# Score products behind another unit's value products, norm weights as a column of x, and a second DMA queue at the start of a streaming-encoder step

## The chip, the cores and the metric

The kernel runs on one core of one Trainium2 chip. The metric is the device time of one execution in microseconds (us); lower is better. The time before is the median of three runs.

## The reference, cut to what matters

One step of a one-layer hybrid encoder: 512 prompt rows and 32 sample rows (544 together) of width 1024, 256 memory tokens, and caches for the sample rows. Three groups of heads, A, B and M, take their queries, keys, values and gates from one input projection, and one output projection joins them.

```python
def _mixer_inputs(x, g, w_in, pos):
    z = _rmsnorm(x, g) @ w_in                       # 1024 x 3880
    qa, ka, va, ga, qb, kb, vb, gb, qm, gm, qi, ki, wi = _split_cols(z)
    qb, kb = _rope(qb, pos), _rope(kb, pos)         # qi, ki too
    return ...

def _attend(q, k, v, bias):                         # A: band + bias; M: memory
    s = jnp.einsum('bqhd,bkhd->bhqk', q, k) * ATTN_SCALE + bias
    return jnp.einsum('bhqk,bkhd->bqhd', jax.nn.softmax(s, axis=-1), v)

def _indexer_scores(qi, ki, wi):                    # B: which keys
    dots = jnp.einsum('bqhd,bsd->bqhs', qi, ki) * (D_IDX ** -0.5)
    return jnp.einsum('bqh,bqhs->bqs', wi * (H_IDX ** -0.5), jax.nn.relu(dots))

def _gather_attend(q, k, v, scores, topk):          # B: over the top-k keys
    top_val, top_idx = lax.top_k(scores, topk)
    ...

def _merge(x, oa, ob, om, ga, gb, gm, w_out):
    o = jnp.concatenate([oa * jax.nn.silu(ga), ob * jax.nn.silu(gb), om * jax.nn.silu(gm)], axis=-1)
    return x + o @ w_out                            # then a last _rmsnorm
```

A and B have six heads of 64 columns, M has four; the indexer has eight heads of 32 and one shared key. B picks 128 keys for a prompt row and 256 for a sample row.

## The kernel before, in words

**Precision and products.** Everything is float32. A large product is made of three products of rounded parts: ACT rounds a block of weights to `wh`, DVE or POOL subtracts to get `wl`, the same is done for x (`xTh`, `xTl`), and TensorE (PE) adds `wh·xTh`, `wl·xTh` and `wh·xTl` in one bank of PSUM. So every block of weights passes through SP's DMA queue (a tile `raw`), ACT (`wh`), and POOL or DVE (`wl`) before PE can use it.

**Stages.** The start loads x turned around (`x_t`, eight blocks of 128 rows by 544 columns) and the first columns of `w_in` (the indexer's, 296 wide, as `raw`), block beside block, in `x_load`, lines 861 to 881. `x_split`, lines 897 to 919, multiplies x by the norm weights `g_mix` and splits it. PE fills the time until the first blocks are there with products of a tile `ones`. `ahead_load` and `ahead_split`, lines 816 to 837, do the same for the block of keys `ka0`. Then the blocks of the input projection follow in the order of `EARLY` and `LATE`. Between them lie the attention units: A's three pairs of heads, M's two, B's three. The output projection comes last, first with the rows of A and M (`oAh`, `oAl`, `oMh`, `oMl`), then with those of B (`oBh`, `oBl`), with the residual (`residual`, line 2139) and the final norm (`settle`, lines 2164 to 2197) behind each block.

**A unit of attention** (`attend`, lines 1986 to 2014) makes the parts of its queries and keys (`q`, `ql`, `k`, `kl`), the scores `k·q`, the softmax in tiles `z`, turns them with PE (`ident`), multiplies by the values (`mix`, `z·va` or `z·vb`), and hands the result on. Scores and value products use PE's array divided into parts of half its rows or columns, as do the sample rows' products with the raw weights (`raw,oS`), which `out_sample`, lines 1709 to 1731, issues; `out_rows` adds their results to `xrS` on DVE.

**What sets the order.** A planner runs while the program is built. It keeps a model of all engines (`Line`), and generators in a heap issue the instructions at modelled times; the order on each engine is fixed from then on. Every instruction passes through `Timed.call`, line 411, so all rows of the profile carry that line, and the tiles' names tell them apart. Three rules matter here. `divided(k, issue)`, lines 491 to 512, collects groups of products for the divided array: a group that is alone waits up to `HOLD` for a second, then all that wait are issued together. A unit takes its places for `z` (`SCORES`, nine in all) before it prepares its keys, and gives them back after its value products:

```python
        yield from line.wait(lambda: places[0] >= k)
        places[0] -= k
        ...
        sc = yield from divided(k, u.begin)
        ...
        o = yield from divided(1, lambda: u.mix(bank()))
        places[0] += k
```

And the subtraction for `wl` goes to POOL unless POOL stands more than 0.5 later than DVE in the model. `START` is the order of the first loads ("x" blocks of x, "w" of weights, "t" the tables, "r" rows of x, "m" memory).

Of the kernel before, what the change touches and what calls it, by code (L numbers as in the profile page):

```python
# [36 lines left out]
START = "xxxwwwwtrrrrrwmmrr"  # L37
SURE = 1.0
SLACK = 1.06
HOLD = 2.0  # L40
LAG = 0.3
# [3 lines left out]
EARLY = ("va", "ka1", "ka2", "mk", "mv", "qa0", "qa1", "ga0", "qa2", "ga1", "ga2", "qm0", "gm0", "qm1", "gm1")  # L45
AHEAD = "ka0"
LATE = ("gb0", "kb0", "kb1", "qb0", "qb1", "kb2", "qb2", "vb", "gb1", "gb2")
# [46 lines left out]
class Line:  # L94
# [4 lines left out]
    def __init__(self):  # L99
        self.clk = {"PE": 1.35, "DVE": 0.7, "ACT": 0.9, "POOL": 1.2, "SP": 0.7}  # L100
# [60 lines left out]
    @staticmethod  # L161
    def lag(of, to):

        if of is None and to == "PE":
            return 0.3
        if of == to or of is None:
            return 0.127 if to == "DVE" else 0.09 if to == "POOL" else 0.0
        return 0.95 if of == "SP" else 0.26 if to == "PE" else 0.2 if of == "PE" else 0.06 if of == "POOL" else 0.15
# [69 lines left out]
    def rate(self):  # L238

        t = self.clk["SP"]  # L240
        return 340e3 if t < 1 else 170e3 if t < 2.3 else 330e3 if t < 7 else 310e3 if 11 < t < 22 else 370e3

    def op(self, eng, op, outs, ins, kw):
# [16 lines left out]
        d = (outs[0].size() * 4 / self.rate() if eng == "SP" else  # L260
# [33 lines left out]
    def begin(self, o, t):  # L294
        last = self.last
        o.start = t
        if o.eng == "SP":
            o.end = max(t + 1.3, last["DMA"]) + o.d
            o.after = {"SP": t + 0.45, "DMA": o.end}
# [12 lines left out]
        self.clk[o.eng] = o.end if o.eng != "SP" else t  # L312
# [29 lines left out]
    def sure(self, *tiles):  # L342

        return When(lambda: max(self.had(x) for x in tiles), SURE + (0.0 if self.now() < 40 else 0.0))
# [95 lines left out]
def hybrid_step(ctx: ExitStack, tc: tile.TileContext, a: dict):  # L440
# [3 lines left out]
    V, G, A, PE, DMA = (Timed(line, n, e) for n, e in (("DVE", nc.vector), ("POOL", nc.gpsimd), ("ACT", nc.scalar),  # L444
                                                       ("PE", nc.tensor), ("SP", nc.sync)))
# [44 lines left out]
    def divided(k, issue):  # L490
# [3 lines left out]
        job = [k, issue, None, False]  # L494
        waiting.append(job)
        end = line.now() + HOLD
        while not job[3]:
            if len(waiting) == 1 and line.now() < end:
                yield min(end, line.soon())
                continue  # L500
# [3 lines left out]
            for j in [job] + [j for j in waiting if j is not job]:  # L504
                if there(j[0]):
# [136 lines left out]

    def w_split():
        for i in range(len(w_list)):
# [26 lines left out]
            if i < 4:  # L671
                for kk in range(2):
                    yield line.at(raw[:, kk, :])
                    rounded(wh[:, kk, :], raw[:, kk, :])
                    yield line.at(wh[:, kk, :]) - 0.2
# [7 lines left out]
            tsub(V if i in WV or 0.5 < line.clk["POOL"] - line.clk["DVE"] else G, wl, raw, f(wh))  # L683
# [124 lines left out]
    gT = [cp.tile([P, NK], F32, name=n) for n in ("g_mix", "g_mem")]  # L808
# [7 lines left out]
    def ahead_load():  # L816
# [3 lines left out]
        DMA.dma_start(raw, w_in[k0 * P:k1 * P, c0:c0 + P].rearrange("(k p) n -> p k n", p=P))  # L820
# [4 lines left out]
    def ahead_split():  # L825
        for c, (k0, k1) in enumerate(CHUNKS):
# [9 lines left out]
            tsub(V if c else V, wl, raw, f(wh))  # L836
# [24 lines left out]
    def x_load():  # L861
# [3 lines left out]
        t = (rp.tile([P, 2, N], F32, tag="xr", name="xr", bufs=3) if c < 3 else  # L865
             cp.tile([P, 2, N], F32, tag="gate1", name="xr"))
# [30 lines left out]
    def x_split():  # L897
        for c in range(NK // 2):
            yield from line.wait(lambda: len(x_raw) > c)
            t = x_raw[c]  # L900
            for kk in range(2):
                yield line.at(t[:, kk, :], gT[0])
                k = 2 * c + kk
                h, l = xTh[k // 4][:, k % 4, :], xTl[k // 4][:, k % 4, :]
                if k < 1:
                    for j in range(2):
                        sl = slice(j * N // 2, (j + 1) * N // 2)
                        yield line.at(t[:, kk, :])
                        A.activation(h[:, sl], t[:, kk, sl], AF.Copy, scale=gT[0][:, k:k + 1])
                        x_half[0] += 1  # L910
                    yield line.at(h) - 0.2
                    V.scalar_tensor_tensor(l, t[:, kk, :], gT[0][:, k:k + 1], f(h), op0=ALU.mult, op1=ALU.subtract)
                else:
                    yield from part(h, l, t[:, kk, :], gT[0][:, k:k + 1])
# [3 lines left out]
            G.tensor_tensor(xF[:, k, :], t[:, :, S:N], gT[0][:, k].unsqueeze(2).broadcast_to([P, 2, T]), op=ALU.mult)  # L918
# [1370 lines left out]
```

## Time and profile before

| what | value |
|---|---|
| median of 3 runs | 340.26 us (340.23 to 340.39) |
| the profiled execution | 340.1 us |
| its span | 338.3 us |
| mean granted clock of PE | 0.998 |
| busy share | PE 98%, DVE 84%, ACT 65%, POOL 49% |
| instructions in the span | 7679 |

The profile is of one execution. Busy time is in us and as a share of the span; the slices cut the span in 40 equal parts, with a digit for tenths of busy time. Weight loads of PE have a row of their own, PEld, and overlap its products. A row of the timeline gives start, length, engine, line, operation, tile written and tile read, and how many instructions it groups; a bracket at its end names the engine's idle time just before it and what ended it. A product's modelled end overlaps the next one's start, so the distance of two starts tells what one takes.

### The profile page before, as it was taken

How to read it: one execution, taken by the hardware profiler on the slowest of the kernel's cores; microseconds unless marked ns; L12 is line 12 of the kernel's file. 1: busy time of each engine (PE TensorE's matmuls, PEld its weight loads, DVE VectorE, ACT ScalarE, POOL GpSimd, SP SyncE). 2: the span in 40 equal slices, each digit the busy share in tenths (PEclk: the TensorE clock that was granted, in tenths of full speed). 3: DMA queues.
4: the chain of work that ended last, by engine and by line, in shares of the span. 5: the costliest groups of instructions: out<-in, count | busy, mean ns of one | idle time of the engine just before them, and what ended most of it. 6: DMA issues, size and time to landing. Idle time of an engine off the chain costs nothing.

```text
span 338.3 us, 7679 instructions
## 1 busy us (share of the span) xinstructions
PE 329.9 (98%) x2785; PEld 296.4 (88%) x2785; DVE 283.2 (84%) x726; ACT 219.9 (65%) x523; POOL 166.1 (49%) x191
## 2 busy tenths in 40 slices
PE   8999999999999999999999999999999999999992
PEld 8979997999998989998999999899998776878682
DVE  3957878698989999699999999999979899865762
ACT  5838787898758786776776755532469446864362
POOL 2326261585453389246257764685338513361542
PEclk9999999999999999999999999999999999999999
DMA  7999763176539412314113343141332977002033
GB/s 219 382 302 344 202 219 105 33 216 160 157 84 304 143 58 58 94 37 136 49 33 74 103 140 97 48 117 42 98 127 65 334 296 273 0 2 95 0 114 152
DMA packets 44725, 46.61 MB, mean 138 GB/s; under 512 B 4400, under 2 KB 36720, under 8 KB 44688
## 3 DMA queue, kind: packets, MB, share of 16 engines
q1 hardware_dynamic: 44688, 46.13, 44.0%
q8 instruction: 22, 0.36, 0.4%
q14 instruction: 15, 0.12, 0.1%
HBM read 39.95 MB, written 6.16 MB: 136 GB/s over the span
## 4 chain that ended last, share of the span: by engine, by line
PE 80%; DVE 9%; issue 4%; POOL 3%; ACT 2%; DMA 1%; POOLq 0%; DVEq 0%; ACTq 0%
PE bank L411 80%; DVE gate L411 1%; DVE ysel L411 1%; DVE m L411 1%; DVE xr L411 1%; DMA raw<-in_w_mem_kv_dram 1%; DVE z L411 1%; DVE KSs L411 1%; POOL wl L411 1%; DVE rot L411 1%; POOL wI L411 1%; POOL rot L411 1%; DVE bi L411 0%; ACT junk L411 0%; POOL rs L411 0%
## 5 line engine op out<-in xcount | busy, mean ns | idle before, releaser
L411 POOL TENSOR_TENSOR wl<-raw,wh 128x512 fp32r<-128x512 f32 (+1 forms) x65 | 90.7, 1398 | 107.3 <-ACT wh L411 105.5
L411 PE MATMUL bank<-xTh,wh 128*128 128x272 f32 x352 | 77.0, 299 | 0.1
L411 ACT ACTIVATE wh<-raw 128x512 fp32r<-128x512 f32 (+3 forms) x85 | 52.0, 619 | 37.2 <-PE bank L411 11.8
L411 PE MATMUL bank<-xTh,wl 128*128 128x272 f32 x352 | 73.0, 288 | 0.0
L411 PE MATMUL bank<-xTl,wh 128*128 128x272 f32 x352 | 72.8, 288 | 0.0
L411 PEld LDWEIGHTS bank<-xTh,wh 128*128 128x128 f32 x352 | 55.6, 189 | 5.2 <-issue 4.1
L411 ACT ACTIVATE z<-z,st 128x128 f32<-128x128 f32 (+3 forms) x78 | 41.0, 549 | 22.9 <-DVE st L411 22.9
L411 PEld LDWEIGHTS bank<-xTh,wl 128*128 128x128 f32 x352 | 55.2, 189 | 0.6 <-issue 0.6
L411 PEld LDWEIGHTS bank<-xTl,wh 128*128 128x128 f32 x352 | 55.2, 188 | 0.5 <-issue 0.5
L411 PE MATMUL bank<-wh,xTh 128*128 128x384 f32 (+1 forms) x88 | 26.9, 336 | 0.0
L411 DVE MAX8 m<-ysel 128x8 f32<-128x256 f32 (+2 forms) x48 | 26.4, 550 | 0.1
L411 PE MATMUL bank<-wh,xTl 128*128 128x384 f32 (+1 forms) x88 | 26.2, 327 | 0.0
L411 PE MATMUL bank<-wl,xTh 128*128 128x384 f32 (+1 forms) x88 | 26.1, 326 | 0.0
L411 DVE MATCH_REPLACE8 ysel<-m,ysel 128x256 f32<-128x256 f32 (+2 forms) x48 | 26.0, 542 | 0.0
L411 DVE SCALAR_TENSOR_TENSOR ysel<-r,wI,ysel 128x256 f32<-128x256 f32 (+2 forms) x21 | 18.6, 885 | 4.2 <-ACT r L411 3.6
L411 ACT ACTIVATE junkS<-ysS,bi 128x1056 int8<-128x1056 f32 x16 | 18.7, 1168 | 4.2 <-DVE bi L411 4.1
L411 PE MATMUL bank<-ident,z 128*128 128x128 f32 (+1 forms) x162 | 21.2, 272 | 0.0
L411 PEld LDWEIGHTS bank<-ident,z 128*128 128x128 f32 (+1 forms) x162 | 17.8, 141 | 2.0 <-issue 0.7
L411 ACT COPY z<-bank 128x512 f32<-128x512 f32 (+2 forms) x31 | 15.2, 517 | 5.5 <-PE bank L411 3.9
L411 ACT ACTIVATE r<-bank 128x512 f32<-128x512 f32 (+3 forms) x30 | 14.0, 485 | 5.8 <-PE bank L411 5.0
L411 PEld LDWEIGHTS bank<-wh,xTh 128*128 128x128 f32 x88 | 15.8, 191 | 0.4 <-issue 0.4
L411 PEld LDWEIGHTS bank<-wl,xTh 128*128 128x128 f32 x88 | 15.7, 188 | 0.0
(286 smaller groups left out, 765.1 us busy)
## 6 DMA issues: line engine op xcount, KB each, us to landing
raw<-in_w_in_dram SPq DMA_DIRECT2D x42, 256.0 KB, 2.9
raw<-in_w_out_dram SPq DMA_DIRECT2D x16, 256.0 KB, 4.1
raw<-in_w_in_dram SPq DMA_DIRECT2D x8, 384.0 KB, 4.0
xr<-in_x_t_dram SPq DMA_DIRECT2D x8, 272.0 KB, 4.3
nat<-in_x_prompt_dram SPq DMA_DIRECT2D x4, 512.0 KB, 5.4
raw<-in_w_mem_kv_dram SPq DMA_DIRECT2D x8, 256.0 KB, 3.1
xr<-in_x_prompt_dram SPq DMA_DIRECT2D x4, 512.0 KB, 6.3
out_dram<-xr SPq DMA_DIRECT2D x4, 512.0 KB, 2.6
```

The costliest lines, as they stand in the source:

```text
L411: return fn(*args, **kw)
```

## The change: what it does

**The start.** `norm_mix_g` is no tensor of its own any more: it stands as a 545th column beside x's 544 in `x_t`, and the scalings read it there. The first `raw` block and the first block of `ka0` are issued on ACT's DMA queue (`DMA2`), not SP's. The first two blocks of x are split in two halves, and the second half of the first one waits until the first `wh` is issued.

**Scores behind value products.** `divided` takes a condition `may`. A unit prepares its queries and keys without having its places; its scores then wait in `divided` until the places are there, and the places are given back when the value products are issued. With `LINK`, value products that scores wait for do not hold for company, and the scores go out right behind them.

**The model and the lists.** The planner gets the second queue and other rates for it; `HOLD` is 3.0, `LAG` 0.5, `SCORES` 8, the margin in the first 40 us 1.5; `EARLY` and `LATE` list the blocks in another order; the sample rows' choice waits for the prompt's picks.

**Engines.** The second half of the rotary step of turned blocks, the subtraction for A's `kl`, and that of `ka0`'s later blocks go to POOL; a `wl` goes to DVE only where POOL is 5.0 later.

```diff
-START = "xxxwwwwtrrrrrwmmrr"
+START = "xxxtwwwwrrrrrwmmrr"
-HOLD = 2.0
-LAG = 0.3
+LINK = True
+HOLD = 3.0
+LAG = 0.5
-LATE = ("gb0", "kb0", "kb1", "qb0", "qb1", "kb2", "qb2", "vb", "gb1", "gb2")
+LATE = ("gb0", "kb1", "qb0", "kb0", "gb1", "qb1", "vb", "qb2", "gb2", "kb2")
...
-    def divided(k, issue):
+    def divided(k, issue, may=lambda: True):
...
-        job = [k, issue, None, False]
+        job = [k, issue, None, False, may]
         while not job[3]:
-            if len(waiting) == 1 and line.now() < end:
+            if not may():
+                yield line.soon()
+                continue
+            if sum(j[4]() for j in waiting) == 1 and line.now() < end and not (LINK and any(j[0] and not j[4]() for j in waiting)):
                 yield min(end, line.soon())
                 continue
...
-                if there(j[0]):
+                if there(j[0]) and j[4]():
...
-            tsub(V if i in WV or 0.5 < line.clk["POOL"] - line.clk["DVE"] else G, wl, raw, f(wh))
+            tsub(V if i in WV or 5.0 < line.clk["POOL"] - line.clk["DVE"] else G, wl, raw, f(wh))
...
-        DMA.dma_start(raw, w_in[k0 * P:k1 * P, c0:c0 + P].rearrange("(k p) n -> p k n", p=P))
+        (DMA if ahead else DMA2).dma_start(raw, w_in[k0 * P:k1 * P, c0:c0 + P].rearrange("(k p) n -> p k n", p=P))
...
-            tsub(V if c else V, wl, raw, f(wh))
+            tsub(G if c else V, wl, raw, f(wh))
...
                 DMA.dma_start(t[:, kk, :], a["x_t"][rows, :])
-                DMA.dma_start(gT[0], a["norm_mix_g"])
-            DMA.dma_start(raw[:, kk, :], w_in[rows, QI:QI + 296])
+            (DMA if c + kk else DMA2).dma_start(raw[:, kk, :], w_in[rows, QI:QI + 296])
...
-                if k < 1:
+                if k < 2:
                     for j in range(2):
...
+                        if k == 0 and j:
+                            yield from line.wait(lambda: w_k[0] or wh_0)
...
-            V.tensor_tensor(t, t, ctab["sin64"][:, sl], op=ALU.mult)
+            G.tensor_tensor(t, t, ctab["sin64"][:, sl], op=ALU.mult)
             yield line.at(t, out) - 0.2
-            least(out, V, G).tensor_tensor(out, t, out, op=ALU.add)
+            G.tensor_tensor(out, t, out, op=ALU.add)
...
-    SCORES = 9
+    SCORES = 8
...
-        yield from line.wait(lambda: places[0] >= k)
-        places[0] -= k
...
-        sc = yield from divided(k, u.begin)
+        def begin():
+            places[0] -= k
+            return u.begin()
+
+        sc = yield from divided(k, begin, lambda: places[0] >= k)
...
-        o = yield from divided(1, lambda: u.mix(bank()))
-        places[0] += k
+        def mix():
+            places[0] += k
+            return u.mix(bank())
+
+        o = yield from divided(1, mix)
...
-        pair = Pair(0, hp, lambda hp=hp: both(split_q(queried[0][:, hp, 0:S], 1.0, G), split_of(natural["ka"][:, hp, 0:S], 1.0, V, "k")), lambda: va)
+        pair = Pair(0, hp, lambda hp=hp: both(split_q(queried[0][:, hp, 0:S], 1.0, G), split_of(natural["ka"][:, hp, 0:S], 1.0, G, "k")), lambda: va)
```

Since the planner sets the order, three places show how it moves. First ACT at the very start of the program, before; `m_73` is a scratch tile, `xTh_79` the rounded x:

```order
L411 ACT_TABLE_LOAD
L411 ACTIVATE m_73<-nhalf 128x1
L411 ACTIVATE xTh_79<-xr,g_mix 128x272 x2
L411 ACTIVATE wh<-raw 128x296
L411 ACTIVATE wh<-raw 128x128
L411 ACTIVATE wh<-raw 128x296
```

ACT at the same place in the changed program:

```order
L412 DMA raw<-in_w_in_dram 128x296
L412 DMA raw<-in_w_in_dram 128x128
L412 ACT_TABLE_LOAD
L412 ACTIVATE m_73<-nhalf 128x1
L412 ACTIVATE xTh_79<-xr 128x272
L412 ACTIVATE wh<-raw 128x296
L412 ACTIVATE xTh_79<-xr 128x272
L412 ACTIVATE wh<-raw 128x128
```

Two loads now stand ahead of all else on ACT, `g_mix` is no longer read, and the first `wh` stands between the two halves of x.

Second PE in the last third of the program, where B's value products (`z,vb`) go out among the blocks of the output projection (`wh,oAh` and its like); before:

```order
L411 MATMUL bank<-wh,oAh 128x512
L411 MATMUL bank<-wh,oAl 128x512
L411 MATMUL bank<-wl,oAh 128x512
L411 MATMUL bank<-z,vb 64x128 x20
L411 MATMUL bank<-wh,oAh 128x512
```

PE at the value products of the same unit in the changed program; `ident,z` turns a softmax tile, `k,q`, `k,ql` and `kl,q` are the next unit's scores:

```order
L412 MATMUL bank<-ident,z 128x128 x4
L412 MATMUL bank<-raw,oS 32x512 x4
L412 MATMUL bank<-z,vb 64x128 x20
L412 MATMUL bank<-k,q 128x128 x2
L412 MATMUL bank<-k,ql 128x128 x2
L412 MATMUL bank<-kl,q 128x128 x2
L412 MATMUL bank<-k,q 128x256 x2
L412 MATMUL bank<-k,ql 128x256 x2
L412 MATMUL bank<-kl,q 128x256 x2
L412 MATMUL bank<-k,q 128x384 x2
```

The unit's value products stood alone between whole-array products; now sample products stand ahead of them and the next unit's scores right behind. Over the whole program whole-array products are left for a divided form 39 times before and 33 times after; the unbroken pieces of one divided form are 49 before and 45 after; whole products follow something else 62 times in both.

Third DVE near the end, where it adds PE's last blocks to the residual (`xr` with a number is one block of 128 rows, `xrS` the sample rows, `ss` the sums of squares, `gf` the weights of the last norm); before:

```order
L411 TENSOR_TENSOR xrS<-bank,xrS 32x512
L411 TENSOR_SCALAR ss<-ss 32x1
L411 TENSOR_TENSOR xr_3872<-bank,xr_3872 128x512
L411 SCALAR_TENSOR_TENSOR xrS<-xrS,ss,gf 32x512
L411 TENSOR_TENSOR xr_3873<-bank,xr_3873 128x512
L411 SCALAR_TENSOR_TENSOR xr_3872<-xr_3872,ss,gf 128x512
```

DVE at the same place in the changed program (`xr_3946` to `xr_3948` and `xr_3960` are the four blocks of prompt rows, the last being the one that ends the program):

```order
L412 TENSOR_TENSOR xrS<-bank,xrS 32x512 x4
L412 TENSOR_TENSOR xr_3946<-bank,xr_3946 128x512
L412 TENSOR_TENSOR xrS<-bank,xrS 32x512 x3
L412 TENSOR_TENSOR xr_3947<-bank,xr_3947 128x512
L412 SCALAR_TENSOR_TENSOR xr_3946<-xr_3946,ss,gf 128x512
L412 TENSOR_TENSOR xrS<-bank,xrS 32x512
L412 TENSOR_SCALAR ss<-ss 32x1
L412 TENSOR_TENSOR xr_3948<-bank,xr_3948 128x512
L412 SCALAR_TENSOR_TENSOR xr_3947<-xr_3947,ss,gf 128x512
L412 SCALAR_TENSOR_TENSOR xrS<-xrS,ss,gf 32x512
L412 TENSOR_TENSOR xr_3960<-bank,xr_3960 128x512
```

The eight sums `xrS` of the last sample products move later, among the last three blocks: 81 products of PE followed the last `raw,oS` before, 63 follow it now.

On POOL, `kl<-ka,k` now stands right behind `ql<-queried,q` for each of A's three pairs, and the instructions go from 147 rows of the order to 169.

More of the change, by code (lines that the diff above doesn't have):

```diff
@@ L99, in __init__ @@
     def __init__(self):
-        self.clk = {"PE": 1.35, "DVE": 0.7, "ACT": 0.9, "POOL": 1.2, "SP": 0.7}
+        self.clk = {"PE": 1.35, "DVE": 0.7, "ACT": 0.9, "POOL": 1.2, "SP": 0.7, "SQ": 0.7}
         self.queue = {e: deque() for e in self.clk}
@@ L167, in lag @@
             return 0.127 if to == "DVE" else 0.09 if to == "POOL" else 0.0
-        return 0.95 if of == "SP" else 0.26 if to == "PE" else 0.2 if of == "PE" else 0.06 if of == "POOL" else 0.15
+        return 0.95 if of in ("SP", "SQ") else 0.26 if to == "PE" else 0.2 if of == "PE" else 0.06 if of == "POOL" else 0.15
     def box(self, x):
@@ L236, in shares, with rate @@
         return op in ("tensor_scalar", "tensor_copy") and len(full) > 0 and outs[0].dtype == F32
-    def rate(self):
-        t = self.clk["SP"]
-        return 340e3 if t < 1 else 170e3 if t < 2.3 else 330e3 if t < 7 else 310e3 if 11 < t < 22 else 370e3
+    def rate(self, eng):
+        t = self.clk[eng]
+        return 340e3 if t < 1 else 250e3 if t < 2.3 else 345e3 if t < 7 else 310e3 if 11 < t < 22 else 370e3
     def op(self, eng, op, outs, ins, kw):
@@ L259, in op @@
                     deps.setdefault(o, False)
-        d = (outs[0].size() * 4 / self.rate() if eng == "SP" else
+        d = (outs[0].size() * 4 / self.rate(eng) if eng in ("SP", "SQ") else
              self.cost(eng, op, outs, ins, kw) * (1.0 if eng == "PE" else SLACK))
@@ L296, in begin @@
         o.start = t
-        if o.eng == "SP":
+        if o.eng in ("SP", "SQ"):
             o.end = max(t + 1.3, last["DMA"]) + o.d
-            o.after = {"SP": t + 0.45, "DMA": o.end}
+            o.after = {o.eng: t + 0.45, "DMA": o.end}
         else:
@@ L311, in begin @@
         o.enter(last)
-        self.clk[o.eng] = o.end if o.eng != "SP" else t
+        self.clk[o.eng] = o.end if o.eng not in ("SP", "SQ") else t
     def events(self):
@@ L342, in sure @@
     def sure(self, *tiles):
-        return When(lambda: max(self.had(x) for x in tiles), SURE + (0.0 if self.now() < 40 else 0.0))
+        return When(lambda: max(self.had(x) for x in tiles), SURE + (0.5 if self.now() < 40 else 0.0))
     def idle(self, eng):
@@ L443, in hybrid_step @@
     line = Line()
-    V, G, A, PE, DMA = (Timed(line, n, e) for n, e in (("DVE", nc.vector), ("POOL", nc.gpsimd), ("ACT", nc.scalar),
-                                                       ("PE", nc.tensor), ("SP", nc.sync)))
+    V, G, A, PE, DMA, DMA2 = (Timed(line, n, e) for n, e in (("DVE", nc.vector), ("POOL", nc.gpsimd), ("ACT", nc.scalar),
+                                                       ("PE", nc.tensor), ("SP", nc.sync), ("SQ", nc.scalar)))
     def pool(stack, name, side):
@@ L641, in hybrid_step @@
     at = {}
+    wh_0 = []
     def w_split():
@@ L807, in hybrid_step @@
     mTl = []
-    gT = [cp.tile([P, NK], F32, name=n) for n in ("g_mix", "g_mem")]
+    g_mem = cp.tile([P, NK], F32, name="g_mem")
     x_raw, x_done, m_raw, m_done, rows_in = [], [0], [], [0], []
@@ L864, in x_load @@
         yield from ()
-        t = (rp.tile([P, 2, N], F32, tag="xr", name="xr", bufs=3) if c < 3 else
-             cp.tile([P, 2, N], F32, tag="gate1", name="xr"))
+        t = (rp.tile([P, 2, N + 1], F32, tag="xr", name="xr", bufs=3) if c < 3 else
+             cp.tile([P, 2, N + 1], F32, tag="gate1", name="xr"))
         if c % 2 == 0:
@@ L924, in m_split @@
             t = m_raw[k // 4][:, k % 4, :]
-            yield max(line.at(t, gT[1]), line.clk["ACT"])
-            yield from part(mTh[k // 4][:, k % 4, :], mTl[k // 4][:, k % 4, :], t, gT[1][:, k:k + 1])
+            yield max(line.at(t, g_mem), line.clk["ACT"])
+            yield from part(mTh[k // 4][:, k % 4, :], mTl[k // 4][:, k % 4, :], t, g_mem[:, k:k + 1])
             m_done[0] += k % 2
@@ L1010, in start @@
                 load_tables(32)
-                DMA.dma_start(gT[1], a["norm_mem_g"])
+                DMA.dma_start(g_mem, a["norm_mem_g"])
         allowed[0] = len(w_list)
@@ L1393, in sample_choice @@
                 V.tensor_scalar(neg, dig, b - 2, old, op0=ALU.logical_shift_left, op1=ALU.bitwise_xor)
-        yield from line.wait(lambda: count["scored"] >= len(TILES) and "kb2" in over)
+        yield from line.wait(lambda: count["scored"] >= len(TILES) and "picks" in over)
         rank = cp.tile([P, NKS], F32, tag="rank", name="rank")
@@ L2238, in _layout @@
     arrays["w_in"] = np.ascontiguousarray(arrays["w_in"][:, cols])
[L2239 removed]
+    g = np.asarray(inputs["norm_mix_g"]).reshape(1, D)
+    arrays["x_t"] = np.ascontiguousarray(np.concatenate([arrays["x_prompt"], arrays["x_sample"], g]).T)
     arrays["mem_t"] = np.ascontiguousarray(arrays["mem_prompt"].T)
```

23 lines of the change are left out of this document (12 added, 11 removed).

## The prediction

> **What bounds the kernel now.** I read the page first, engines and slices, then the chain, then the waits of PE, and last the timeline of the start, of one stretch of the middle and of the end.
>
> ```profile
> span 338.3 us, 7679 instructions
> PE 329.9 (98%) x2785; PEld 296.4 (88%) x2785; DVE 283.2 (84%) x726; ACT 219.9 (65%) x523; POOL 166.1 (49%) x191
> ...
> PE   8999999999999999999999999999999999999992
> ...
> PE 80%; DVE 9%; issue 4%; POOL 3%; ACT 2%; DMA 1%; POOLq 0%; DVEq 0%; ACTq 0%
> ```
>
> PE is busy in every slice but the last, and 80% of the chain that ends last is PE's own work. PE's list of waits, beside one of 1.0 us for the tile `ones` before it begins, has two entries (columns: us in total, times, longest):
>
> ```profile
> PE bank L411 <- DVE KSs L411: 0.5, 1, 0.5
> PE bank L411 <- ACT bf_ok L411: 0.4, 1, 0.4
> ```
>
> So 0.9 us is all that shorter waits of PE can give between its first and its last product. The rest of the time can change in four ways: PE starts earlier, has fewer pauses between its products, is made to wait anew, or what follows its last product changes length. The sum is made against the profiled execution, 340.1 us: a span of 338.3 and 1.8 around it. That is 0.16 under the median of 340.26. About 0.7 us, 0.2%, is what a measurement here can tell from no change.
>
> **The change part by part: the start.** In the timeline of before (columns: start, length, engine, what, in brackets the idle time before it and what ended it):
>
> ```profile
> 0.73 0.38 SPq L411 DMA_DIRECT2D xr<-in_x_t_dram  x1
> 1.05 4.64 PE L411 MATMUL bank<-ones 128*128 128x128 f32 x20 [1.05 <-DVE ones L411]
> 1.16 0.42 SPq L411 DMA_DIRECT2D g_mix<-in_norm_mix_g_dram  x1
> 1.63 1.37 SPq L411 DMA_DIRECT2D raw<-in_w_in_dram  x3
> 3.04 0.43 SPq L411 DMA_DIRECT2D xr<-in_x_t_dram  x1
> 3.79 0.93 ACT L411 ACTIVATE xTh<-xr,g_mix 128x272 fp32r<-128x272 f32 x2 [1.57 <-DMA g_mix<-in_norm_mix_g_dram]
> 4.85 1.15 ACT L411 ACTIVATE wh<-raw 128x296 fp32r<-128x296 f32 x3
> 5.36 0.91 PE L411 MATMUL bank<-wh,xTh 128*128 128x296 f32 x3
> 6.11 0.58 PE L411 MATMUL bank<-wl,xTh 128*128 128x296 f32 x3
> 6.82 0.75 ACT L411 ACTIVATE xTh<-xr,g_mix 128x544 fp32r<-128x544 f32 x1 [0.81 <-DMA xr<-in_x_t_dram]
> 7.68 0.62 PE L411 MATMUL bank<-wh,xTh 128*128 128x296 f32 x3
> ```
>
> From issue to landing, for the first load of `x_t` and the first of `w_in` (columns after the size: us):
>
> ```profile
> xr<-in_x_t_dram SPq DMA_DIRECT2D x1, 272.0 KB, 2.8
> raw<-in_w_in_dram SPq DMA_DIRECT2D x1, 148.0 KB, 3.2
> ```
>
> Before, ACT waits for `g_mix`, splits two halves of x, and then rounds the first `wh` at 4.85, just when its raw rows land (1.63 + 3.2 = 4.83); PE follows 0.51 later, at 5.36. After, the norm weights come with x's rows, so that wait of ACT goes, and the first raw load is issued by ACT itself at about 0.73, 0.90 earlier, beside x's. x lands at 0.73 + 2.8 = 3.5; ACT's half takes 0.47 and ends at 4.0; the raw rows land at 0.73 + 3.2 = 3.9 at best. Both loads now share the DMA engines from their first byte, for which I add 0.2: `wh` at 4.2, PE at 4.7, 0.65 earlier. The warm-up has 8 products of `ones` for 10: four fifths of its 4.31 us (5.36 - 1.05) end at 4.5 and are not late. What is late next is the second block of x, whose rounding ends at 7.57 for a product at 7.68; its load goes out at about 1.63 for 3.04 and moves by more than PE does.
>
> All of the 0.65 is not won: the first three products took 0.91, the next three 0.58, so products that come earlier still run at the slow rate, at 0.58/0.91 = 0.64 of the later speed or below. I take −0.4 (0 to −0.9, the whole of the raw load's shift).
>
> The Trainium skill (TensorE: Matmul & The Clock Gate, Part 1) says that the array runs at half its clock until a window of about 3.4 us was busy, whenever that window begins. The two rows agree in kind; by its half, an estimate, 0.65 earlier would be worth 0.33 at most.
>
> The Trainium skill (DMA: Bandwidth & Descriptors, Issuing engines are not separate DMA queues) speaks against the second queue: transfers of all engines interleave on the same 16 DMA engines, and issuing from several saves only the issuing time. By it the gain would be the two issues that stood ahead of the raw load, which by the rows are the 0.90 of 1.63 − 0.73 that I use; what it takes back is in my 0.2.
>
> **Visits to the divided array.** Score, value and sample products use the array in parts. The order on PE has 33 entries from whole-array products into such forms where it had 39, and 45 unbroken pieces of one such form for 49: scores now stand right behind another unit's value products. What an entry and a piece cost shows in the timeline of PE:
>
> ```profile
> 263.21 0.39 PE L411 MATMUL bank<-wh,oAl 128*128 128x512 f32 x1
> 263.44 0.40 PE L411 MATMUL bank<-wl,oAh 128*128 128x512 f32 x1
> 263.77 2.40 PE L411 MATMUL bank<-z,vb 128*64 128x128 f32 x40
> 266.10 0.50 PE L411 MATMUL bank<-wh,oAh 128*128 128x512 f32 x1
> 266.44 0.39 PE L411 MATMUL bank<-wh,oAl 128*128 128x512 f32 x1
> ...
> 128.58 1.09 PE L411 MATMUL bank<-z,va 128*64 128x128 f32 x16
> 129.60 0.18 PE L411 MATMUL bank<-bf_ok,over 128*128 128x1 bf16 x1
> ```
>
> Whole products start 0.23 apart (263.21 to 263.44), the step into the divided form takes 0.33: an entry costs 0.10. 40 rows take 2.33 (263.77 to 266.10), 16 take 1.02 (128.58 to 129.60): 0.0546 a row, and 2.33 − 40 × 0.0546 = 0.15 that does not depend on the count. The first whole product after a piece takes 0.34 for 0.23, but that return is made 62 times before and after, as the order has it, since transposes stand between. So the gain is 6 × 0.10 + 4 × 0.15 = 1.2. At least the entries alone, 0.6; at most 6 × (0.10 + 0.15 + 0.11) = 2.2 if each visit saved is whole. I take −1.2. The two PE waits of 0.9 above I leave standing: their causes are a choice step and a test that the change does not shorten.
>
> **The end.** The last eight products of sample rows, `raw,oS`, stand 81 products before PE's last one in the order of before, 63 in that of after: 18 × 0.23 = 4.1 us later. Their sums, `xrS`, are DVE's.
>
> ```profile
> 313.61 1.93 PE L411 MATMUL bank<-raw,oS 128*32 128x512 f32 x16
> 314.82 2.12 DVE L411 TENSOR_TENSOR xrS<-bank,xrS 32x512 f32<-32x512 f32 x3 [0.60 <-PE bank L411]
> ...
> 328.68 0.75 DVE L411 SCALAR_TENSOR_TENSOR xr<-xr,ss,gf 128x512 f32<-128x512 f32 x1 [1.09 <-POOL ss L411]
> 329.35 0.68 DVE L411 TENSOR_TENSOR xr<-bank,xr 128x512 f32<-128x512 f32 x1
> ...
> 330.92 1.28 POOL L411 TENSOR_TENSOR xr<-xr,gf 128x512 f32<-128x512 f32 x1 [2.27 <-ACT sq L411]
> 331.54 0.28 PE L411 MATMUL bank<-wl,oBh 128*128 128x256 f32 x1
> 331.86 0.43 DVE L411 TENSOR_TENSOR xr<-bank,xr 128x256 f32<-128x256 f32 x1 [0.82 <-PE bank L411]
> ...
> 333.00 0.55 POOL L411 TENSOR_TENSOR ss<-ss,nhalf 128x1 f32<-128x1 f32 x1 [0.64 <-DVE ss L411]
> 333.58 0.72 ACT L411 ACTIVATE xr<-xr,ss 128x512 f32<-128x512 f32 x1 [2.10 <-POOL ss L411]
> ```
>
> I walk DVE's list of after with these lengths. From the last `raw,oS` to PE's end there are 63 products of 0.2 (a few are narrow), 12.2 us. In that time DVE has eight `xrS` sums of 2.12/3 = 0.71, four other sums of 0.68, three scalings of 0.75 and two short steps: 5.7 + 2.7 + 2.2 + 0.2 = 10.8, so the sum of the last block's first half ends 1.4 before PE's last product does. Before it ends at 330.03, 1.8 before PE's end at 331.82. It is 0.4 later, and POOL's `xr,gf` behind it (1.28) pushes the `ss` that releases the last ACT step: +0.5. Between 0 (if DVE finds the sums early) and +1.5 (if POOL's product ends only after it would have started `ss`).
>
> **Work moved to POOL.**
>
> ```profile
> L411 POOL TENSOR_TENSOR wl<-raw,wh 128x512 fp32r<-128x512 f32 (+1 forms) x65 | 90.7, 1398 | 107.3 <-ACT wh L411 105.5
> L411 POOL TENSOR_TENSOR ql<-queried,q 128x512 fp32r<-128x512 f32 x5 | 6.5, 1292 | 0.0
> L411 DVE TENSOR_TENSOR kl<-ka,k 128x512 fp32r<-128x512 f32 x3 | 2.5, 831 | 0.0
> ```
>
> POOL gets 22 instructions more, at most 22 × 1.29 = 28 us, and has 105.5 us in which it only waits for `wh`: nothing, as long as those that PE needs soon (`kl`, the rope products) are not queued. DVE loses as much and bounds nothing in the middle. All else that moves (longer holds, the orders of blocks, one place less for z) acts on the order that is counted above. The sum: 340.1 − 0.4 − 1.2 + 0.5 = 339.0.
>
> **The rivals.** *More than that.* The start counts in full (−0.65), the end costs nothing, and the 0.9 of waits goes: 339.0 − 0.25 − 0.5 − 0.9 = 337.3. For it: z is free earlier. Against it: those waits are not for z.
>
> *Nothing.* The two loads at the start slow each other and PE starts as before, the end costs 1.2: 340.1 − 1.2 + 1.2 = 340.1. For it: the x3 of raw loads landed while x's second block was still waited for 0.81 (the row at 6.82).
>
> *The clock.* The warm-up, shortened to end at 4.5, leaves a gap before the first product. If such a gap makes PE begin its slow time anew, as long as before (1.05 to about 5.95), 4.9 us run at 0.64 of the speed and lose 4.9 × 0.36 = 1.8, and the start's gain: 339.0 + 0.4 + 1.8 = 341.2. Against it: a gap of 0.2. The Trainium skill (TensorE: Matmul & The Clock Gate, Part 1) has the window free-running, so a short gap can fall on either side of it; no run here shows that yet.
>
> *Slower: POOL is late.* Pair A's three `kl` leave DVE (0.83) and stand behind `ql` on POOL, so the scores' last operand is ready 1.3 later than `ql`, three times. PE's order is fixed: where the product `kl,q` comes up first, all of PE stands. The point is a backlog on POOL of over 1.3 us when PE reaches the scores; two of three so, 2 × 1.3 = 2.6: 341.6. For it: `ql` and `kl` directly follow each other in POOL's order. Against it: POOL is 49% busy, and the scores may wait while other products go.
>
> **How the numbers follow.** The forecast has 0.55, with its own range 338.3 to 339.9 (the start −0.4, the visits up to −1.4 and the end nothing at one side, the start −0.1, the visits −0.9 and the end +0.8 at the other); 0.46 of it lies more than 0.7 below 340.1, 0.09 within. More than that 0.15, nothing 0.12, the clock 0.07, POOL late 0.11. Faster: 0.46 + 0.15 = 0.61. Same: 0.09 + 0.12 = 0.21. Slower: 0.07 + 0.11 = 0.18. The range from 337.0 to 341.2 takes in all but POOL's case and the outer ends of the bounds.
>
> **What would show it.** Right: ACT's first `xTh` without a wait for norm weights and PE's first `wh,xTh` near 4.7; the step from `z,vb` to `k,q` below 0.15 with no whole product between; PE's waits under 1.5 us in all; from PE's last product to the span's end 0.5 more than the 6.5 of before (338.3 − 331.82). Wrong: PE at 5.2 or later (the start), waits of PE for `kl` or `rq` (POOL), the first products at 0.3 each beyond 7 us (the clock), or a middle that is as long as before although the visits are fewer.

## The result, and the profile after

| | before | changed |
|---|---|---|
| median | 340.39 us (5 runs, 340.23 to 340.57) | 338.78 us (5 runs, 338.11 to 339.12) |
| ratio | | 0.9948, interval 0.9933 to 0.9962 |
| the profiled execution | 340.1, span 338.3 | 338.11, span 336.3 |

The changed kernel is 1.6 us faster by the medians and 2.0 by the two profiled executions; timed again beside the later experiments it had 338.24, ratio 0.9939 (0.9926 to 0.9951). The forecast was 339.0, 1.1 less than the profiled 340.1. The sums below are made between the two profiled executions; that of the changed kernel is the fastest of its five, so a second profile of it, at 338.24 (span 336.45), stands beside it where it differs.

From the page of the changed kernel, span, engines, slices and chain:

```profile
span 336.3 us, 7695 instructions
PE 327.3 (97%) x2781; PEld 296.0 (88%) x2781; DVE 269.7 (80%) x696; ACT 218.8 (65%) x527; POOL 194.1 (58%) x221
PE   8999999899999999999999999999999999999991
PE 91%; DVE 3%; ACT 2%; issue 1%; POOL 1%; POOLq 0%; ACTq 0%
```

PE is still the bound, and more of the chain is its own work: 91% for 80%. POOL has 28 us more and DVE 13.5 less, and neither shows as a wait of PE. PE's list of waits, beside the 1.0 for `ones`:

```profile
PE bank L412 <- ACT ysS L412: 0.9, 1, 0.9
PE bank L412 <- DVE zS L412: 0.2, 1, 0.2
```

Two waits of 0.9 in all went (for `KSs` and `bf_ok`) and two of 1.1 came. The start, in the timeline:

```profile
0.72 0.89 ACTq L412 DMA_DIRECT2D raw<-in_w_in_dram  x2
0.73 0.38 SPq L412 DMA_DIRECT2D xr<-in_x_t_dram  x1
3.80 0.52 ACT L412 ACTIVATE xTh<-xr 128x272 fp32r<-128x272 f32 x1 [0.66 <-DMA xr<-in_x_t_dram]
4.23 0.43 ACT L412 ACTIVATE wh<-raw 128x296 fp32r<-128x296 f32 x1
4.57 0.51 ACT L412 ACTIVATE xTh<-xr 128x272 fp32r<-128x272 f32 x1
4.71 1.03 PE L412 MATMUL bank<-wh,xTh 128*128 128x296 f32 x3
5.11 0.79 DVE L412 SCALAR_TENSOR_TENSOR xTl<-xr,xTh 128x544 fp32r<-128x544 f32 x1
5.58 0.58 PE L412 MATMUL bank<-wl,xTh 128*128 128x296 f32 x3
6.00 0.63 PE L412 MATMUL bank<-wh,xTl 128*128 128x296 f32 x3
6.47 0.41 PE L412 MATMUL bank<-xTh,wh 128*128 128x272 f32 x2
```

PE's first product is at 4.71 for 5.36, 0.65 earlier, as the forecast had it. But the second product needs the second half of x, which ACT now rounds behind the first `wh` and ends at 5.08; it starts at 5.13. The seventh needs `xTl`, which DVE begins behind that half and ends at 5.90. The tenth product, `xTh,wh`, is at 6.47, 0.46 earlier than in the timeline of before:

```profile
6.93 0.42 PE L411 MATMUL bank<-xTh,wh 128*128 128x272 f32 x2
```

In the second profile of the changed kernel PE starts at 4.85, 0.51 earlier, and its tenth product is at 6.64, 0.29 earlier.

In the middle, the value products of the unit that the order showed, with the next unit's scores behind them:

```profile
257.33 1.06 PE L412 MATMUL bank<-raw,oS 128*32 128x512 f32 x8
258.33 2.40 PE L412 MATMUL bank<-z,vb 128*64 128x128 f32 x40
260.66 0.33 PE L412 MATMUL bank<-k,q 64*128 64x128 f32 x2
```

The distance from the value products to the scores is 2.33, exactly that to the whole product behind 40 rows before (263.77 to 266.10). So the last step, 2.33 − 39 × 0.0546 = 0.20, costs the same whether scores or whole products follow, and the 0.15 or less that the prediction gave as a sign did not come; what is saved is that the scores need no entry of their own from whole products. From PE's first to its last product it is 324.7 us for 326.5.

The end, last rows of the timeline:

```profile
327.27 0.67 DVE L412 TENSOR_TENSOR xr<-bank,xr 128x512 f32<-128x512 f32 x1
327.79 0.73 ACT L412 ACTIVATE xr<-xr,ss 128x512 f32<-128x512 f32 x1 [0.51 <-POOL ss L412]
328.42 0.61 ACT L412 ACTIVATE sq<-xr 128x512 f32<-128x512 f32 x1
329.10 0.28 PE L412 MATMUL bank<-wl,oBh 128*128 128x256 f32 x1
329.20 1.26 POOL L412 TENSOR_TENSOR xr<-xr,gf 128x512 f32<-128x512 f32 x1 [1.45 <-ACT sq L412]
331.22 0.55 POOL L412 TENSOR_TENSOR ss<-ss,nhalf 128x1 f32<-128x1 f32 x1 [0.61 <-DVE ss L412]
331.81 0.72 ACT L412 ACTIVATE xr<-xr,ss 128x512 f32<-128x512 f32 x1 [2.14 <-POOL ss L412]
```

DVE's sum of the last block's first half ends at 327.94, 1.44 before PE's end (329.38); it was 1.8 before it. Between it and POOL's `xr,gf` stands ACT's `sq`: before, it began 0.08 behind DVE's sum; now it begins 0.48 behind, since ACT is still scaling the block before it (327.79), for which POOL's `ss` came late. So POOL's `xr,gf` starts 0.18 before PE's end, it was 0.90, and the last ACT step 2.43 behind PE's end, it was 1.76. From PE's end to the span's end it is 6.9 us for 6.5; from the last ACT step on it is 4.53 for 4.75.

Together: 0.46 at the first ten products, 1.98 between the tenth and PE's end, and 0.44 given back at the end: 338.3 − 0.46 − 1.98 + 0.44 = 336.3. In the second profile the three are 0.29, 2.04 and 0.45.

### The profile page after: what moved, and what is told of

It reads as the page before. It is cut to its first block, busy times and chain, and to the rows that moved or that the text cites. A ratio compares the mean times of both kernels' runs of the same rounds, so it can differ in the third digit from the quotient of the medians.

```text
span 336.3 us, 7695 instructions
## 1 busy us (share of the span) xinstructions
PE 327.3 (97%) x2781; PEld 296.0 (88%) x2781; DVE 269.7 (80%) x696; ACT 218.8 (65%) x527; POOL 194.1 (58%) x221
## 4 chain that ended last, share of the span: by engine, by line
PE 91%; DVE 3%; ACT 2%; issue 1%; POOL 1%; POOLq 0%; ACTq 0%
PE bank L412 91%; DVE xrS L412 1%; DVE xr L412 1%; POOL ss L412 1%; ACT junk L412 1%; ACT sq L412 0%; ACT r L412 0%; DVE zS L412 0%; POOL xr L412 0%; POOLq L2284 0%; DVE vaS L412 0%; ACT wh L412 0%; DVE mTl L412 0%; DVE ysS L412 0%; ACT mTh L412 0%
## 5 line engine op out<-in xcount | busy, mean ns | idle before, releaser
L412 POOL TENSOR_TENSOR wl<-raw,wh 128x512 fp32r<-128x512 f32 (+3 forms) x74 | 100.8, 1369 | 68.4 <-ACT wh L412 67.2
L412 ACT ACTIVATE z<-z,st 128x256 f32<-128x256 f32 (+3 forms) x79 | 41.2, 548 | 20.4 <-DVE st L412 20.3
L412 DVE SCALAR_TENSOR_TENSOR ysel<-r,wI,ysel 128x256 f32<-128x256 f32 (+2 forms) x21 | 19.7, 940 | 6.1 <-ACT r L412 5.1
L412 PE MATMUL bank<-ident,z 128*128 128x128 f32 (+1 forms) x162 | 20.2, 271 | 0.0
L412 DVE TENSOR_TENSOR xr<-bank,xr 128x512 f32<-128x512 f32 (+1 forms) x17 | 11.1, 655 | 6.1 <-PE bank L412 5.9
```

Source lines behind the costliest of these rows:

```text
L412: return fn(*args, **kw)
```

## The experiments

The theory: PE's own list of work is what the time consists of, and the change saves visits to the divided array, half a microsecond at the start, and loses some at the end. The first rival says that the direct follow-up itself (`LINK`) is what saves time; others, that the lists of blocks, the moved subtractions or the second queue do. Every kernel was timed in three or five rounds against the kernel before; the ratio is to that. Where an edit makes the planner build another order, the text says from which of the changed kernel's 1282 rows PE's order differs. A step is the time from the start of one product to the start of the next. Three sums over the trace are used: what PE's steps between forms take beyond its usual pace, and the same for its other steps, those over 0.5 us (long) apart from the short ones. The changed kernel has 13.1, 1.05 and 31.5, the kernel before 14.9, 1.1 and 31.4.

**LINK off.**

```diff
-LINK = True
+LINK = False
```

> The changed kernel with LINK off, all else as it is: PE's order still has 33 entries into divided forms and 45 pieces, the last sample products stand 72 products before the end instead of 63. If the number of visits decides, 338.8 as the changed kernel has, or up to 0.3 less by the tail. If the direct follow-up of scores behind value products is what saves the time, it loses the 1.2 of the forecast: 340.0.

Measured 337.73, ratio 0.9921 (0.9909 to 0.9933). The entries and pieces are the same 33 and 45; PE's order is the same up to row 1022 of 1282. So the rule that brings scores and value products together is not `LINK`: with the places taken at the time of issue, groups that wait are gathered anyway. In that kernel, at the same place:

```profile
257.41 2.40 PE L412 MATMUL bank<-z,vb 128*64 128x128 f32 x40
259.75 1.06 PE L412 MATMUL bank<-raw,oS 128*32 128x512 f32 x8
260.74 0.33 PE L412 MATMUL bank<-k,q 64*128 64x128 f32 x2
```

Here the samples stand between, at no cost. From its first to its last product PE takes 324.6 us, as in the changed kernel; the end is 6.3 for 6.9. That is 0.6, all that the two profiled executions differ (335.7 and 336.3). The medians differ by more, and the part over 0.6 lies within the spread of the runs. The start of this run, with the same products in the same order, bears on the forecast too:

```profile
1.05 3.48 PE L412 MATMUL bank<-ones 128*128 128x128 f32 x16 [1.05 <-DVE ones L412]
4.85 0.96 PE L412 MATMUL bank<-wh,xTh 128*128 128x296 f32 x3 [0.32 <-ACT wh L412]
```

Here PE reached its later pace within the warm-up (the last `ones` are 0.11 apart, not 0.21). Still the second product waits for x's second half (at 5.26, ACT's rounding ends at 5.21), and the first to the tenth product take 1.75 (4.85 to 6.60), as in the changed kernel (1.76). Before it was 1.57.

**Places taken first, as before.** `attend` and `divided` of before, with SCORES 9 and HOLD 2.

```diff
+        yield from line.wait(lambda: places[0] >= k)
+        places[0] -= k
...
-        sc = yield from divided(k, begin, lambda: places[0] >= k)
+        sc = yield from divided(k, u.begin)
...
```

> The changed kernel with attend and divided of before (places taken ahead of the preparation, SCORES 9, HOLD 2): 41 entries and 47 pieces for 33 and 45. If visits decide, 8 x 0.10 + 2 x 0.15 = 1.1 slower by the terms of the forecast, 8 x 0.36 = 2.9 if each visit counts whole: 339.9 to 341.7. If the lists of blocks or the moved subtractions bring the gain, 338.8.

Measured 347.22, ratio 1.0198 (1.0183 to 1.0213). That is neither theory's number. The eight more visits cost what was expected of them, 1.1 to 2.9: the steps between forms take 14.7 us for 13.1. But the long steps make 6.2 for 1.05, and the short ones 1.6 more. PE's list of waits shows where they come from:

```profile
PE bank L412 <- ACT wh L412: 1.6, 1, 1.6
PE bank L412 <- DVE z L412: 1.2, 3, 0.5
PE bank L412 <- DVE cacheM L412: 1.2, 1, 1.2
```

PE's order differs from row 46 on. The order built anew makes PE wait for `wh` and `cacheM`, which the edit does not touch.

**The two first loads on SP's queue.** The planner's model stays as it is, so PE's order is the same row for row.

```diff
-                                                       ("PE", nc.tensor), ("SP", nc.sync), ("SQ", nc.scalar)))
+                                                       ("PE", nc.tensor), ("SP", nc.sync), ("SQ", nc.sync)))
```

> The changed kernel with the two first loads on SP's queue in place of ACT's; PE's order is the same, row for row. If the second queue matters by its earlier issue, the first raw rows are issued at about 1.16 for 0.72 and PE starts 0.4 later: 339.2. If the norm column alone gives the start, PE starts at 4.7 as it does and the time is 338.8. If sharing the engines costs more than the issue saves, it is faster than 338.8.

Measured 339.02, ratio 0.9959 (0.9946 to 0.9971). The start in the timeline:

```profile
1.17 1.36 SPq L412 DMA_DIRECT2D raw<-in_w_in_dram  x3
4.09 0.43 ACT L412 ACTIVATE wh<-raw 128x296 fp32r<-128x296 f32 x1
4.58 1.27 PE L412 MATMUL bank<-wh,xTh 128*128 128x296 f32 x3
5.65 0.94 PE L412 MATMUL bank<-wl,xTh 128*128 128x296 f32 x3
6.99 0.41 PE L412 MATMUL bank<-xTh,wh 128*128 128x272 f32 x2
```

The raw rows were issued 0.45 later and rounded 0.14 earlier: PE's first product is at 4.58. In the eleven profiles that have the new start with both queues it lies between 4.71 and 5.07, so the second queue brings nothing to the first product; the norm column (no wait of its own) and one queue do as well. What is 0.2 slower by the median, and 1.0 in the profile (a span of 337.3), comes behind: PE keeps its slower first pace until about 6.9, which costs 0.52 by the tenth product (6.99 for 6.47), and later blocks lose the rest. The slower pace is the subject of the last section; the rest, some 0.4 of one profile, bounds what the second queue may be worth further on.

**The start alone.** The kernel before with the norm column, the halves of x, the second queue and the order of the first loads.

```diff
-START = "xxxwwwwtrrrrrwmmrr"
+START = "xxxtwwwwrrrrrwmmrr"
...
-            DMA.dma_start(raw[:, kk, :], w_in[rows, QI:QI + 296])
+            (DMA if c + kk else DMA2).dma_start(raw[:, kk, :], w_in[rows, QI:QI + 296])
...
```

> The kernel before with the start of the change alone (norm column, halves of x, second queue, order of the first loads): 41 entries and 48 pieces for 39 and 49. If the start adds in full, PE starts 0.64 earlier and the time is 340.4 - 0.6 + 0.2 - 0.15 = 339.8. If the earlier start is lost at a later wait, 340.4. If only half of it counts, as forecast, 340.1.

Measured 347.2, ratio 1.0199 (1.0177 to 1.022). PE's first product is at 4.90, 0.46 earlier than before, and the re-planned rest has 4.7 us of long steps for 1.1, and 2.0 more in short ones and 1.3 more between forms than the kernel before. Again the number belongs to the new order and not to the step tested.

**A visit more, twenty times,** against **the same work without a visit.** Ahead of every later part of a unit's value products stands a small product, overwritten at once, over the whole array in the one kernel and in the divided form in the other.

```diff
+                if i:
+                    PE.matmul(o[:, i * P:i * P + 32], ident, ident[:, 0:32], start=True, stop=True)
                 for b in range(n // P):
```

```diff
+                if i:
+                    PE.matmul(o[0:64, i * P:i * P + 32], ident[:, 0:64], ident[:, 0:32], start=True, stop=True,
+                              tile_position=(0, 0))
                 for b in range(n // P):
```

> The changed kernel with a small product over the whole array (ident by 32 of its columns, overwritten at once) ahead of every later part of a unit's value products, 20 in all: 56 entries and 67 pieces. Set against the kernel with the same small product in the divided form (36 entries, 48 pieces), 20 entries x 0.10 + 19 pieces x 0.15 = 4.9 slower by the forecast's terms, 20 x 0.36 = 7.2 if the return counts too. If entries are hidden by other work, the two are within 0.5 of each other.

> The control: the changed kernel with 20 small products ahead of the later parts of the value products, but in the divided form, so that the array's form does not change: 36 entries and 48 pieces for 33 and 45, 20 x 0.05 = 1.0 of work, 3 x (0.10 + 0.15) = 0.75 of visits: 340.5.

Measured 348.27, ratio 1.0232 (1.0208 to 1.0256), and the control 342.07, ratio 1.0045 (1.0027 to 1.0062). The difference is 6.2 us for 20 visits, 0.31 each. One unit shows the price without the rest. With visits, and with the same small products inside the form:

```profile
120.50 0.44 PE L412 MATMUL bank<-z,va 128*64 128x128 f32 x4
120.87 0.41 PE L412 MATMUL bank<-ident 128*128 128x32 f32 x2
...
122.94 0.67 PE L412 MATMUL bank<-keysA,queried 64*32 64x272 f32 x12
```

```profile
120.57 0.44 PE L412 MATMUL bank<-z,va 128*64 128x128 f32 x4
...
122.26 0.68 PE L412 MATMUL bank<-keysA,queried 64*32 64x272 f32 x12
```

The same 24 rows and two small products take 2.44 us with two visits more and 1.69 without: 0.375 a visit. The entries are not hidden; the higher of the two prices of the forecast, 0.36 with the return, is the nearer one. The control itself is 1.6 above its expectation, with 1.4 more of long steps than the changed kernel: its order, too, was built anew. The kernel with the visits has no such steps, so without the control's 1.4 the difference would be 7.6, or 0.38 a visit, an estimate that agrees with the one unit.

**The rule alone in the kernel before.**

```diff
-    def divided(k, issue):
+    def divided(k, issue, may=lambda: True):
...
-    SCORES = 9
+    SCORES = 8
...
```

> The kernel before with the rule alone (divided with its condition, places taken at issue, LINK, SCORES 8, HOLD 3): PE's order has 40 entries and 48 pieces for 39 and 49. If visits decide, 340.4 + 0.10 - 0.15 = 340.4, no gain: the rule needs the lists. If the direct follow-up itself saves time, 339.2.

Measured 346.57, ratio 1.0181 (1.016 to 1.0203). With 40 entries for 39 the rule saves no visit there, as the theory of visits has it, but its time is neither number: it has 3.8 us of long steps for 1.1, 1.0 more between forms and 2.1 more in short ones.

**The last sample products at once.**

```diff
-            ps = yield from divided(len(rows), issue)
+            if at_ == 8:
+                yield from room(len(rows))
+                ps = issue()
+            else:
+                ps = yield from divided(len(rows), issue)
```

> The changed kernel with the last group of sample products issued as soon as its operands and banks are there, without company: 33 entries and 45 pieces as before, but 78 products stand behind it where 63 did. If DVE's late sums cost the 0.4 at the end, the end is 6.5 behind PE's last product for 6.9 and the time 338.4. If the end is set by something else, 338.8.

Measured 337.73, ratio 0.9917 (0.9901 to 0.9934). PE's order is the same up to row 1201 of 1282, and its first to last product take the same 324.7. The end:

```profile
326.83 0.69 DVE L412 TENSOR_TENSOR xr<-bank,xr 128x512 f32<-128x512 f32 x1 [1.43 <-PE bank L412]
328.42 1.29 POOL L412 TENSOR_TENSOR xr<-xr,gf 128x512 f32<-128x512 f32 x1 [1.96 <-ACT sq L412]
329.32 0.28 PE L412 MATMUL bank<-wl,oBh 128*128 128x256 f32 x1
331.35 0.72 ACT L412 ACTIVATE xr<-xr,ss 128x512 f32<-128x512 f32 x1 [2.09 <-POOL ss L412]
```

DVE has its sum 2.1 before PE's end where it had it 1.4 before, in fact waits 1.43 for PE, POOL starts 1.2 before PE's end, and the last ACT step comes 1.75 behind PE's end for 2.43. The end is 6.3 for 6.9. So the late sample products, with DVE's sums and the steps of POOL and ACT behind them, are what the change gave back, 0.6 and not only 0.4.

**The changed kernel once more, and three on the same chip.**

> The changed kernel once more, as a measure beside the three others of this group: 338.8, and spans that differ by up to 1 us among its runs, by when PE's first products reach their full rate. If that rate has nothing to do with the spread, the rate sets in at the same time in every profile.

Measured 338.24 (338.09 to 338.95), ratio 0.9939 (0.9926 to 0.9951). The rate does not set in at the same time: in this profile PE's products change pace at about 5.7, in the first one at about 5.4, with the same products in the same order.

```diff
-LINK = True
+LINK = False
...
+            if at_ == 8:
+                yield from room(len(rows))
+                ps = issue()
...
```

> The changed kernel without LINK and with the last sample products issued at once: 33 entries, 45 pieces, 87 products behind the last sample ones. If only the end was open, it ends 6.3 behind PE's last product as the two kernels with 72 and 78 did, and the time is 337.7: no gain from the second of two steps for the same wait. If the two steps add, 337.1.

Measured 337.61, ratio 0.992 (0.9907 to 0.9934), with the end at 6.3: the two do not add. It is 0.6 below the changed kernel on the same chip, and within 0.2 of either step alone, which the spread of the runs does not tell apart.

```diff
-EARLY = ("va", "qa0", "ka1", "mk", "qa1", "mv", "ga0", "ka2", "qa2", "ga1", "ga2", "qm0", "gm0", "qm1", "gm1")
+EARLY = ("va", "ka1", "ka2", "mk", "mv", "qa0", "qa1", "ga0", "qa2", "ga1", "ga2", "qm0", "gm0", "qm1", "gm1")
-LATE = ("gb0", "kb1", "qb0", "kb0", "gb1", "qb1", "vb", "qb2", "gb2", "kb2")
+LATE = ("gb0", "kb0", "kb1", "qb0", "qb1", "kb2", "qb2", "vb", "gb1", "gb2")
...
-        yield from line.wait(lambda: count["scored"] >= len(TILES) and "picks" in over)
+        yield from line.wait(lambda: count["scored"] >= len(TILES) and "kb2" in over)
```

> The changed kernel with the EARLY and LATE lists of before, and the choice waiting for kb2 again: 34 entries and 46 pieces for 33 and 45. If the rule brings the fewer visits and the lists only their company, 338.8 + 0.3 - 0.5 (90 products behind the last sample ones) = 338.6. If rule and lists were fitted to each other, PE waits as it did with the parts undone before: 343 to 347.

Measured 345.4, ratio 1.0143 (1.0122 to 1.0164). The long steps make 6.4, and PE waits as with the other parts undone:

```profile
PE bank L412 <- POOL wl L412: 2.3, 1, 2.3
PE bank L412 <- DVE st L412: 1.4, 1, 1.4
```

```diff
-        pair = Pair(0, hp, lambda hp=hp: both(split_q(queried[0][:, hp, 0:S], 1.0, G), split_of(natural["ka"][:, hp, 0:S], 1.0, G, "k")), lambda: va)
+        pair = Pair(0, hp, lambda hp=hp: both(split_q(queried[0][:, hp, 0:S], 1.0, G), split_of(natural["ka"][:, hp, 0:S], 1.0, V, "k")), lambda: va)
```

> The changed kernel with pair A's kl subtraction on DVE again: 34 entries and 47 pieces for 33 and 45, 78 products behind the last sample ones. If POOL was never late for kl, 338.8 + 0.1 + 0.3 - 0.6 = 338.6, and PE has no wait for kl in either. If POOL's backlog costs time, it is faster than 338.2.

Measured 345.5, ratio 1.0154 (1.0139 to 1.0169). Three subtractions of 0.83 us on DVE cannot cost 7. PE's order is that of the changed kernel up to row 446 and differs from there on, and there PE waits:

```profile
PE bank L412 <- DVE o L412: 1.3, 2, 1.1
PE bank L412 <- ACT z L412: 1.2, 1, 1.2
PE bank L412 <- ACT bf_ok L412: 1.2, 1, 1.2
PE bank L412 <- DVE bi L412: 0.9, 1, 0.9
```

None of these is `kl`. Neither the changed kernel nor this one shows a wait of PE for `kl`, so the rival in which POOL is late did not come about; what `kl` costs on DVE or POOL by itself stays unmeasured, since the change of plan covers it.

## Why the prediction was right, point by point

**The start, −0.4: right in size, not in its reason.** PE's first product moved by the 0.65 that was worked out, and 0.46 of it was left at the tenth product; in the second profile it was 0.51 and 0.29, so the exact 0.65 has luck in it. The forecast took the loss for the slow pace of the first products. But the run with `LINK` off had the later pace before its first product and needed as long for the first ten, 1.75 for 1.76. What holds PE there is a term that the forecast did not have: the change itself puts x's second half behind the first `wh`, and the second product and `xTl` wait for it. The part credited to the earlier issue on ACT's queue was not there: with both loads on SP's queue the raw rows were rounded no later (4.09 and 4.23). What the change removed is the wait for `g_mix` and the place of the second half of x ahead of `wh`.

**The visits, −1.2: right in kind, too small.** PE's steps between forms took 14.9 us beyond its usual pace before (88 steps) and take 13.1 after (78): −1.8, inside the range of 0.6 to 2.2. The step that was mis-sized is the return: the forecast put it at nothing because whole products follow something else 62 times in both orders. Most of those 62 are returns from transposes and the like, which keep the array whole; the returns from a divided form fell from 39 to 33, by the same six as the entries, and they took 10.0 us and take 8.0, some 0.26 each against 0.09 for an entry. The 0.15 that was counted by pieces is a part of that return. Returns −2.0, entries −0.6, and +0.8 for the direct steps between forms, 12 for 10, make the −1.8; the two kernels with twenty small products put the visit at 0.31 to 0.375. The first whole product behind a return, 0.34 for 0.23 in the forecast's rows, was left out for the same reason; such products took 3.2 us beyond the pace before and take 2.8. Which part of the change brings the fewer visits is not separated: `LINK` does not, and the rule without the lists, or the lists of before with the rule, gave orders with other waits.

**The end, +0.5: right, with two errors that cancel in part.** Measured +0.44, by the path that was walked: DVE's sum 1.4 before PE's end as worked out, POOL's `xr,gf` later, `ss` later. But the walk left out ACT, whose late scaling adds 0.4 between the sum and POOL, so that the last ACT step comes 0.67 later; and what follows that step is 0.22 shorter, for a cause that stays open. Undoing the late samples alone gives 0.6.

**POOL's work at nothing: right** for this order. The 22 of the forecast are rows of the order, and a row can stand for several instructions: by the two pages POOL has 30 more (221 for 191). Their 28.0 us are what the bound of 28 allowed, by luck, since they are shorter than the 1.29 that was put on each. POOL's wait for ACT, 105.5 before, is what they went into:

```profile
L412 POOL TENSOR_TENSOR wl<-raw,wh 128x512 fp32r<-128x512 f32 (+3 forms) x74 | 100.8, 1369 | 68.4 <-ACT wh L412 67.2
```

**The waits of PE, left standing: right in sum alone.** The two that were to stay went, 0.9 in all, and two others came, 1.1; that they balance is luck.

Together −0.46 − 1.98 + 0.44 = −2.0 in the profiled executions for the −1.1 of the forecast; the 0.9 between is the visits, 0.6, the 0.4 of the products behind a return, 0.1 at start and end, and 0.2 back in small shifts of PE's pace.

**What the forecast did not see** is how near the order stands to a worse one. It took the order as given, and so it could count; but five kernels that undo or do one part of the change (places first, the start alone, the rule alone, the old lists, `kl` on DVE) all came out between 345.4 and 347.2, 5 to 7 slower than the kernel before and 7 to 9 slower than the changed one. PE's long steps, many of them waits at places far from the part, make 2.7 to 6.8 us of that; short steps and more visits make the rest. The parts can't be added up from such runs. That the two complete versions have few waits because their lists and constants were fitted to each other is argued from this, not shown; what in the planner's model misses by a microsecond or more was not tried. The edits that leave the order alone, or alone up to its last fifth (one queue, LINK off, the last samples), gave clean answers.

## What to carry to other kernels

Where a planner sets the whole order, an experiment answers for one part only if the order elsewhere stays the same: change the real queue and not the model, change a step near the end, or put equal work in two forms, and compare the orders before the times. Count returns to the whole array with the entries: here a visit to a divided form cost a third of a microsecond, and the step out of the value products 0.20 whatever came next. Work that is moved late for company's sake is to be checked against what ends last: eight small sums near the end, on DVE and in the steps behind them, cost 0.6.

## What was not expected of the hardware

PE's first products run at little more than half their later rate, until a moment that is not set by the program. With the rule alone in the kernel before, PE starts where it did before, at 5.34 for 5.36, behind the same warm-up products:

```profile
5.34 1.09 PE L412 MATMUL bank<-wh,xTh 128*128 128x296 f32 x3
6.22 0.94 PE L412 MATMUL bank<-wl,xTh 128*128 128x296 f32 x3
```

Before, the same two rows were at 5.36 and 6.11, and the second took 0.58. Here three products still take 0.94 at 6.22, 0.25 from start to start where 0.135 is the later pace; the pace changes at about 7.2, in the kernel before by 5.8. Six profiles share PE's order of the changed kernel at least up to row 1022: there the pace changes between about 4.2 (`LINK` off, within the warm-up) and 6.9 (one queue), and at 5.4 and 5.7 in the two of the changed kernel itself. The granted clock in the profile does not show it. With one queue, the table by stages (stretch, length, busy time of PE, PEld, DVE, ACT and POOL, clock, share of the DMA engines, GB/s):

```profile
5.50:6.60 1.10, 1.10 (x6) 1.10 (x5) 0.67 (x3) 0.63 (x2) 0.00 (x0) 1.00 1.16 342
```

Its clock column says 1.00 for a stretch in which products of 0.135 took 0.25. The Trainium skill (TensorE: Matmul & The Clock Gate, Part 1) tells of a clock gate that halves the rate until PE was busy through a window of its own that runs free of the program, so that the same kernel changes pace at another moment in each run. The rows agree: with the same products in the same order, the pace changed between 4.2 and 6.9 us. Half the rate for the 1.4 us from 5.8 to 7.2 is 0.7 us of work, an estimate of the size of the spread among the changed kernel's runs (338.09 to 339.12); that it is the cause of that spread is argued, since only the profiled runs show the pace. In the five of the six profiles where it changed by 5.7 the first ten products took 1.74 to 1.79, in the one with 6.9 2.41: only a late change costs. In the forecast this was the clock's rival, put down to a gap in the warm-up; it needs no gap, and the gap of 0.32 with `LINK` off did not bring the slow pace back (the third to sixth product are 0.13 to 0.14 apart).
